# A two-layer diffusion trunk on one core: the second attention's context norm goes behind the first k product, the latent sums two tiles later, and the halves of the final norm get tiles of their own

## The chip, the cores and the metric

The kernel runs on one core of a Trainium2 chip. The metric is device time in microseconds (us) of one execution. TensorE (PE) does the matrix products, VectorE (DVE) and ScalarE (ACT) the elementwise work, GpSimd (POOL) a few additions and multiplications and some transfers, and SyncE (SP) issues most transfers. Each engine works through its own list of instructions in order; between engines an instruction waits for semaphores.

## The reference

512 latent tokens and 256 context tokens of 1024 features pass two layers. A layer is a modulated RMS norm, an attention with a gated residual, a second modulated norm, and a SwiGLU feed-forward part (2816 hidden) with a gated residual. The second layer gives no context out, so there the context is only normed and projected to keys and values. The output is the latent stream after a final RMS norm.

```python
def rmsnorm(x, g):
    y = xf * lax.rsqrt(jnp.mean(xf * xf, axis=-1, keepdims=True) + NORM_EPS)
    return y * g
...
h_x = modulate(rmsnorm(x, norm_g[layer, 0]), mod_x[0], mod_x[1])
h_c = modulate(rmsnorm(ctx, norm_g[layer, 0]), mod_c[0], mod_c[1])
...
    q_x, k_x, v_x = jnp.split(h_x @ w_in, [C_Q_COLS, C_Q_COLS + C_KV_COLS], axis=-1)
        kv_c = h_c @ w_in[:, C_Q_COLS:]
...
    x = x + mod_x[5] * swiglu(h_x, ffn_w1[layer], ffn_w3[layer], ffn_w2[layer])
return rmsnorm(x, final_g)
```

## The kernel before

Features lie on the 128 partitions, tokens along the row: a stream of 1024 features is eight tiles (KT = 8), 128 x 512 for the latents (`xr`, later `x1`) and 128 x 256 for the context (`cr`). For precision every operand of a large product is split into a high and a low part (`hb` holds both of a normed tile, `wh` and `wl` those of a weight tile), and a product is three matmuls per tile of the contraction (`mm3`, L205, lines L207 to L209). ACT makes the high part of a weight by a cast, DVE the low part by a subtraction.

Around the change three pieces of work follow each other.

*The end of the first feed-forward part* (`down_last`, L1301). PE makes eight latent tiles, then eight context tiles, each 128 x 256 from 12 matmuls (L1281 to L1283). DVE adds each to its residual (`to_residual`, L1275). After the third context tile (`m == 2`) `next_norm` (L1162) is written, the latents' norm: squares on ACT (L329, L332), additions on DVE (L338) and POOL (L336) into two running tiles `ns_a`, a sum over the partitions on PE by a matmul with ones (L309), then Ln, Exp and Square on ACT (L313, L315, L316) between three small operations on DVE (L314, L317, L318). `h_make` (L345) then gives each of the eight tiles its scale (L350, DVE), shift and high part (L351, ACT) and low part (L352, DVE). Behind the last context tile the same norm is written for the context, in six slices of one tile `q`, sums and `h_make` included.

*The beginning of the second attention* (from L1404). `k_x(0)` makes the first two key heads of the latents (24 matmuls of 512 columns from `hb`, L207 to L209); `v_part` makes the values, first of the latents (`g` = 1, 2), then of the context (`g` = 0), as 128 x 256 matmuls (L396 to L398); `k_c(0)` makes the first context keys, and `k_x(1)`, `k_c(1)` the rest. The weight tiles come in the order that `weights0` (L540) writes: `w_c[8]` for the first keys and `w_c[10]`, `w_c[11]` for the values, then `w_c[9]` for the other keys. Those of 8 and 10 are split right behind the last hidden tile (`behind_g`, L529); `w_c[11]` is split as usual. There are three buffers for split weight tiles, so `w_c[9]` is split when one of the first three is done with.

*The end of the kernel* (the second `down_last`, L1726). The output is made in two halves of 256 tokens: eight tiles of the first half, then eight of the second (12 matmuls each, lines L207 to L209), each added to its residual by DVE (L1693). `final_norm(0)` (L1712) is written behind the third tile of the second half, `final_norm(1)` behind the last. A final norm squares and sums like the others, multiplies each tile by its gain on ACT (L1720, into `fo`), and, when 1/rms is there, multiplies `fo` by it, five tiles on DVE and three on POOL (L1723), and stores them (L1724). Both final norms take their tiles from the same small set of tags of one pool (`npool`, L1568).

The order in which engines meet this work is not the order of the text: a scheduler places each instruction in the list of its engine at build time, by the text's order as priority and its own estimate of when the inputs are there. `tc.issue_after(z)` makes it place an instruction behind `z`; the chip itself does not wait there. Once placed, the lists are fixed.

## Time and profile before

| | |
|---|---|
| runs (3) | 1646.57, 1652.71, 1653.13 us; median 1652.71 us |
| profiled execution, its own time | 1649.52 us |
| its span, first to last instruction | 1647.7 us |
| PE busy | 1567.5 us (95%), 10222 matmul records |
| DVE busy | 1251.1 us (76%) |
| ACT busy | 749.2 us (45%) |
| POOL busy | 272.6 us (17%) |
| mean granted TensorE clock | 0.989 |
| HBM read, written | 160.45 MB, 4.86 MB |

Times in the profile count from the first instruction, so the span ends at 1647.7 us, and 1.8 us of the execution's own time lie around it. A row of the timeline gives start and duration, the engine, the line, what is written from what, and in brackets how long the engine had been idle before and what released it. A matmul's duration contains the time to drain; matmuls that follow each other start closer together than their durations say. The granted clock is 1.00 at full speed.

### The profile page before, as it was taken

Reading aid. Unit: us, or ns where it says so; the run is one execution under the profiler, and the core shown is the slowest. Engines: PE = TensorE matmul, PEld = TensorE weight load, DVE = VectorE, ACT = ScalarE, POOL = GpSimd, SP = SyncE. Lnnn points to the kernel's source line nnn. Section 1 sums busy time; section 2 is a strip of 40 time slices with the busy share of each in tenths; the row PEclk is TensorE's granted clock in tenths of the full one; section 3 lists DMA queues with packets and bytes.
Section 4 is the critical chain, followed back from the end, with each engine's and each line's share of the span. In section 5 each row is a group of like instructions: output and inputs, shape, how many; then the busy total and the mean of one; then the engine's idle time right before and its main releaser. Section 6 shows DMA issues by size and latency. Waiting matters only on the chain.

```text
span 1647.7 us, 26339 instructions
## 1 busy us (share of the span) xinstructions
PE 1567.5 (95%) x10222; PEld 1402.1 (85%) x10222; DVE 1251.1 (76%) x2155; ACT 749.2 (45%) x1326; POOL 272.6 (17%) x313
## 2 busy tenths in 40 slices
PE   5999998999999899999999998999999999999996
PEld 3798887877888789999999996977788799989896
DVE  4758698976576888879798879587665987869685
ACT  4446554556244423333434254356655552525243
POOL 2222222345010000010100001254322000000001
PEclk9999999999999999999999999999999999999998
DMA  9323254644225556675766762411010432323321
GB/s 340 100 58 89 80 157 131 189 133 119 69 64 131 155 163 160 159 199 159 193 182 170 201 173 94 101 54 40 14 39 25 156 128 78 127 74 95 120 73 52
DMA packets 69508, 199.52 MB, mean 121 GB/s; under 512 B 6932, under 2 KB 19380, under 8 KB 69384
## 3 DMA queue, kind: packets, MB, share of 16 engines
q1 hardware_dynamic: 59464, 164.40, 32.1%
q0 software_dynamic: 9344, 32.92, 9.4%
q8 instruction: 81, 1.33, 0.3%
q10 hardware_dynamic: 576, 0.52, 0.1%
q14 instruction: 43, 0.35, 0.1%
HBM read 160.45 MB, written 4.86 MB: 100 GB/s over the span
## 4 chain that ended last, share of the span: by engine, by line
PE 58%; issue 7%; DMA 6%; DVE 6%; ACT 2%; POOL 0%; DVEq 0%; SPq 0%; POOLq 0%; ACTq 0%
PE f L1250 4%; PE f L1251 4%; PE f L1249 4%; PE f L1653 4%; PE f L1652 4%; PE f L1651 4%; PE f L1281 3%; PE f L1282 3%; PE f L1283 3%; DMA wl<-raw 2%; PE lin L207 2%; PE t L1485 2%; PE lin L208 2%; PE lin L209 2%; PE f L1705 2%
## 5 line engine op out<-in xcount | busy, mean ns | idle before, releaser
L196 ACT ACTIVATE wh<-raw 128x1024 fp32r<-128x1024 f32 (+1 forms) x94 | 90.2, 976 | 233.9 <-DVE raw L500 124.4
L207 PE MATMUL lin<-hb,wh 128*128 128x512 f32 (+1 forms) x456 | 161.3, 354 | 8.5 <-DVE q L369 2.2
L208 PE MATMUL lin<-hb,wh 128*128 128x512 f32 (+1 forms) x456 | 159.4, 349 | 0.1
L209 PE MATMUL lin<-hb,wl 128*128 128x512 f32 (+1 forms) x456 | 158.3, 347 | 0.0
L197 DVE TENSOR_TENSOR wl<-raw,wh 128x1024 fp32r<-128x1024 f32 (+1 forms) x94 | 104.7, 1119 | 34.7 <-ACT wh L196 32.6
L269 DVE SCALAR_TENSOR_TENSOR junk<-raw,tables 128x1024 bf16<-128x1024 f32 x80 | 97.6, 1220 | 20.1 <-DMA raw<-in_ada_wT_dram 19.8
L202 POOL DMA_DIRECT2D wl<-raw x41 | 35.7, 871 | 458.6 <-ACT wl L201 421.6
L1281 PE MATMUL f<-g,wh 128*128 128x512 f32 (+1 forms) x304 | 103.4, 342 | 6.0 <-DVE q L1263 5.0
L207 PEld LDWEIGHTS lin<-hb,wh 128*128 128x128 f32 x456 | 86.1, 189 | 22.8 <-issue 3.0
L159 DVE TENSOR_TENSOR wl<-raw,wh 128x1024 fp32r<-128x1024 f32 x62 | 81.4, 1313 | 29.8 <-ACT wh L158 27.0
L1282 PE MATMUL f<-g,wh 128*128 128x512 f32 (+1 forms) x304 | 103.4, 341 | 0.0
L1283 PE MATMUL f<-g,wl 128*128 128x256 f32 (+1 forms) x304 | 101.9, 338 | 1.2 <-DMA wl<-raw 1.2
L1652 PE MATMUL f<-hb,wh 128*128 128x256 f32 x360 | 101.7, 283 | 0.0
L1651 PE MATMUL f<-hb,wh 128*128 128x256 f32 x360 | 101.4, 283 | 0.0
L1653 PE MATMUL f<-hb,wl 128*128 128x256 f32 x360 | 101.2, 283 | 0.0
L158 ACT CAST wh<-raw 128x1024 fp32r<-128x1024 f32 x62 | 64.9, 1047 | 77.5 <-PE lin L208 23.6
L1250 PE MATMUL f<-hb,wh 128*128 128x384 f32 x288 | 96.3, 335 | 1.1 <-DVE hb L197 1.1
L1249 PE MATMUL f<-hb,wh 128*128 128x384 f32 x288 | 96.4, 335 | 0.7 <-ACT hb L196 0.7
L1251 PE MATMUL f<-hb,wl 128*128 128x384 f32 x288 | 96.3, 334 | 0.3 <-DMA wl<-raw 0.3
L208 PEld LDWEIGHTS lin<-hb,wh 128*128 128x128 f32 x456 | 86.3, 189 | 11.0 <-issue 0.9
L209 PEld LDWEIGHTS lin<-hb,wl 128*128 128x128 f32 x456 | 86.2, 189 | 10.3 <-issue 0.3
L336 POOL TENSOR_TENSOR ns_a<-ns_a,ns_s 128x256 f32<-128x256 f32 (+1 forms) x16 | 17.3, 1084 | 442.7 <-ACT ns_s L332 434.4
(397 smaller groups left out, 4953.7 us busy)
## 6 DMA issues: line engine op xcount, KB each, us to landing
raw<-in_w_dram SPq DMA_DIRECT2D x132, 512.0 KB, 3.8
raw<-in_ada_wT_dram SPq DMA_DIRECT2D x80, 512.0 KB, 4.2
wl<-raw POOLq DMA_DIRECT2D x41, 512.0 KB, 6.4
raw<-in_w_ab_dram SPq DMA_DIRECT2D x24, 512.0 KB, 4.4
raw<-in_ada_w_dram SPq DMA_DIRECT2D x16, 512.0 KB, 9.5
k<-k SPq DMA_DIRECT2D x16, 384.0 KB, 6.0
raw<-in_w_c_dram SPq DMA_DIRECT2D x12, 512.0 KB, 4.3
nb<-in_na_bias_dram POOLq DMA_DIRECT2D x16, 256.0 KB, 3.8
```

The costliest lines, as they stand in the source:

```text
L207: nc.tensor.matmul(ps, wh(k), xh(k), start=k == 0, stop=False)
L208: nc.tensor.matmul(ps, wh(k), xl(k), start=False, stop=False)
L209: end = nc.tensor.matmul(ps, wl(k), xh(k), start=False, stop=k == n - 1)
L1249: nc.tensor.matmul(ps, wh(k), b[:, 0, :], start=k == 0, stop=False)
L1250: nc.tensor.matmul(ps, wh(k), b[:, 1, :], start=False, stop=False)
L1251: nc.tensor.matmul(ps, wl(k), b[:, 0, :], start=False, stop=k == 3)
L1281: nc.tensor.matmul(ps, hi, g[:, 0, cols[v]], start=first, stop=False)
L1282: nc.tensor.matmul(ps, hi, g[:, 1, cols[v]], start=False, stop=False)
L1283: nc.tensor.matmul(ps, lo, g[:, 0, cols[v]], start=False, stop=last)
L1651: nc.tensor.matmul(ps, wh(k), b[:, 0, :], start=k == 0, stop=False)
L1652: nc.tensor.matmul(ps, wh(k), b[:, 1, :], start=False, stop=False)
L1653: nc.tensor.matmul(ps, wl(k), b[:, 0, :], start=False, stop=k == 3)
```

## The change

Three things are moved; no operation is added or left out.

1. `next_norm` is written after the fifth context tile (`m == 4`), not the third. Its sums on PE come two tiles (24 matmuls) later.
2. Of the context's norm only squares and additions stay in `down_last`; their two running tiles lie in a residual buffer that is free by then (`spool0`). The sum on PE, 1/rms and `h_make` are written behind `k_x(0)`, with tiles of the attention's own pool. The split of `w_c[11]` gets its place behind the fourth latent `h_make`.
3. `final_norm` is cut in two. What multiplies by 1/rms and stores is now `put_out`, and `put_out(0)` is placed behind the last residual addition. The second half's norm gets its running tiles and its 1/rms from another pool (`spool`, tag `sum`), not from those of the first half.

```diff
-    def behind_g(raw):
+    def behind(act, dve, raw):
         hi, lo = S.part_tiles()
-        with tc.issue_after(g_made[0].ins):
-            nc.scalar.copy(hi, raw[0])
-        with tc.issue_after(g_made[1].ins):
-            nc.vector.tensor_sub(lo, raw[0], f32(hi))
+        with tc.issue_after(act.ins):
+            nc.scalar.copy(hi, raw)
+        with tc.issue_after(dve.ins):
+            nc.vector.tensor_sub(lo, raw, f32(hi))
         return hi, lo
...
         for j in (8, 10):
-            S.add_made([w_c[j]], behind_g)
-        for j in (11, 9, 0, 1, 2, 3, 4, 5, 6, 7):
+            S.add_made([w_c[j]], lambda raw: behind(*g_made, raw[0]))
+
+        S.add_made([w_c[11]], lambda raw: behind(*h_made[3 - KT], raw[0]))
+        for j in (9, 0, 1, 2, 3, 4, 5, 6, 7):
             S.add(w_c[j])
...
-                if m == 2:
+                if m == 4:
                     next_norm()
             q = q_tile()
-            pool = Carve([q[:, NC * i : NC * i + NC] for i in range(6)])
-            r = rstd_of(fps(), sq_sum(cr, pool), D, pool)
-            for k in range(KT):
-                h_make(k, hc[k], cr[k], r, 1, 0, 1, pool)
+            sums = [spool0[0][:, NC * i : NC * i + NC] for i in range(2)]
+            c_sums.extend(sq_sum(cr, Carve(sums + [q[:, NC * i : NC * i + NC] for i in range(2)])))
...
         k_x(0, w0)
+        r = rstd_of(linp(), c_sums, D, npool)
+        for k in range(KT):
+            h_make(k, hc[k], cr[k], r, 1, 0, 1, npool)
         wv = [tuple(wslice(t, 256) for t in S.next(1 - i)) for i in range(2)]
...
-        fo = []
+        fo, gains = [], []
+
+        def norm_tiles(i):
+            a = (spool[0], "sum", 2) if i else (fp, "s", 2)
+            return PoolMap(ns_a0=a, ns_a1=a, ns_s=(fp, "q", 2), ns_v=(fp, "s", 2), ns_y=a, ns_t=(fp, "s4", 1))
...
-            r = rstd_of(fps(), sq, D, npool)
+            gains.append((ts, rstd_of(fps(), sq, D, pool)))
+
+        def put_out(i):
+            ts, r = gains[i]
             for k in range(KT):
                 (nc.gpsimd if k in (1, 4, 7) else nc.vector).tensor_mul(ts[k], ts[k], r)
-                (nc.scalar if i and k % 2 else nc.sync).dma_start(out[:, k, c], ts[k])
+                (nc.scalar if i and k % 2 else nc.sync).dma_start(out[:, k, halves[i]], ts[k])
...
                     if ci and m == 2:
                         final_norm(0)
+            with tc.issue_after(end.ins):
+                put_out(0)
             final_norm(1)
+            put_out(1)
```

What the scheduler makes of it differs from before at two places only.

The first is PE's list at the step from the feed-forward part to the second attention. `f<-q,ones` is the context's sum and `hb_124`, `hb_125` are the first two of the eight normed tiles; L1282, L1283 are the last down product. Before:

```order
L1282 MATMUL f<-g,T 128x256
L1283 MATMUL f<-g,T 128x256
L309 MATMUL f<-q,ones 128x256 x2
L207 MATMUL t<-hb_124,wh 128x512
L208 MATMUL t<-hb_124,wh 128x512
L209 MATMUL t<-hb_124,wl 128x512
L207 MATMUL t<-hb_125,wh 128x512
L208 MATMUL t<-hb_125,wh 128x512
```

The changed kernel has from the same place on (line numbers are its own: L399 to L401 are the value matmuls, L312 the sum):

```order
L1290 MATMUL f<-g,T 128x256
L207 MATMUL t<-hb_124,wh 128x512
L399 MATMUL t<-wh,hb_124 128x256 x2
L208 MATMUL t<-hb_124,wh 128x512
...
L208 MATMUL t<-hb_125,wh 128x512
L209 MATMUL t<-hb_125,wl 128x512
...
L401 MATMUL t<-wl,hb_125 128x256
L312 MATMUL lin<-res,ones 128x256 x2
L207 MATMUL t<-hb_126,wh 128x512
```

The context's sum has moved from ahead of the first key matmul to behind the second normed tile, and the value matmuls of that tile, which stood behind the keys, are now mixed in: each normed tile is used by nine matmuls (three for keys, six for values) before the next is asked for. Further on, the values of the context stand among the first context keys, so the last 14 matmuls ahead of `k_x(1)` begin where `w_c[10]` is last read; before, 36 stood there.

The second place is DVE's list at the end of the kernel. `res` is the residual addition of one output tile, `ns_a` an addition of squares, `fo` the multiplication by 1/rms. Before:

```order
L318 SCALAR_TENSOR_TENSOR ns_y<-ns_t,ns_y 128x256
L1693 SCALAR_TENSOR_TENSOR res<-f,mod_117,res 128x256
L338 TENSOR_TENSOR ns_a<-ns_a,ns_s 128x256
L1723 TENSOR_TENSOR fo<-fo,ns_y 128x256 x5
L1693 SCALAR_TENSOR_TENSOR res<-f,mod_117,res 128x256
L338 TENSOR_TENSOR ns_a<-ns_a,ns_s 128x256
L1693 SCALAR_TENSOR_TENSOR res<-f,mod_117,res 128x256
L338 TENSOR_TENSOR ns_a<-ns_a,ns_s 128x256
L314 TENSOR_SCALAR ns_v<-f 128x256
```

In the changed kernel:

```order
L321 SCALAR_TENSOR_TENSOR ns_y<-ns_t,ns_y 128x256
L1701 SCALAR_TENSOR_TENSOR res<-f,mod_117,res 128x256
L341 TENSOR_TENSOR ns_a<-ns_a,ns_s 128x256
L1701 SCALAR_TENSOR_TENSOR res<-f,mod_117,res 128x256
L1740 TENSOR_TENSOR fo<-fo,ns_y 128x256 x5
L317 TENSOR_SCALAR ns_v<-f 128x256
```

The five multiplications of the first half stood ahead of the last two residual additions; they now stand behind the last one, ahead of the second half's `ns_v`. POOL's list has changed in the same way: its two additions for the second half now come ahead of its three multiplications for the first.

More of the change, by code (lines that the diff above doesn't have):

```diff
@@ L303, in load_rows @@
             nc.gpsimd.dma_start(cs[v], crow_dram[v : v + 1, :].to_broadcast([P, D]))
+    h_made = []
     def rstd_of(ps, accs, dim, pool):
@@ L351, in h_make @@
         act = nc.scalar.activation(h[:, 0, :], t, AF.Identity, bias=b, scale=1.0)
-        nc.vector.scalar_tensor_tensor(h[:, 1, :], t, b, f32(h[:, 0, :]), op0=ALU.add, op1=ALU.subtract)
+        h_made.append((act, nc.vector.scalar_tensor_tensor(h[:, 1, :], t, b, f32(h[:, 0, :]), op0=ALU.add, op1=ALU.subtract)))
         return act
@@ L564, in weights0 @@
         for j in (8, 10):
-            S.add_made([w_c[j]], behind_g)
-        for j in (11, 9, 0, 1, 2, 3, 4, 5, 6, 7):
+            S.add_made([w_c[j]], lambda raw: behind(*g_made, raw[0]))
+        S.add_made([w_c[11]], lambda raw: behind(*h_made[3 - KT], raw[0]))
+        for j in (9, 0, 1, 2, 3, 4, 5, 6, 7):
             S.add(w_c[j])
     spool0, tpool, small_parts = [], [], []
+    c_sums = []
     ada1 = [(l, s_, k) for l, s_ in [(0, 5)] + [(1, z) for z in range(6)] for k in range(KT)]
@@ L1692, in to_residual @@
         def to_residual(m, ps, c):
-            nc.vector.scalar_tensor_tensor(x1[m][:, c], ps, mod[1][:, 5, 0, m : m + 1], x1[m][:, c], op0=ALU.mult, op1=ALU.add)
+            return nc.vector.scalar_tensor_tensor(x1[m][:, c], ps, mod[1][:, 5, 0, m : m + 1], x1[m][:, c], op0=ALU.mult, op1=ALU.add)
         def down(js):
@@ L1708, in down @@
                     to_residual(4 * i + m, ps[m], slice(0, NX))
-        fo = []
+        fo, gains = [], []
+        def norm_tiles(i):
+            a = (spool[0], "sum", 2) if i else (fp, "s", 2)
+            return PoolMap(ns_a0=a, ns_a1=a, ns_s=(fp, "q", 2), ns_v=(fp, "s", 2), ns_y=a, ns_t=(fp, "s4", 1))
         def final_norm(i):
             c = halves[i]
-            sq = sq_sum([x1[k][:, c] for k in range(KT)], npool, apart=i == 1)
+            pool = norm_tiles(i)
+            sq = sq_sum([x1[k][:, c] for k in range(KT)], pool, apart=i == 1)
             ts = []
@@ L1735, in down_last @@
                     )
-                    to_residual(m, ps, c)
+                    end = to_residual(m, ps, c)
                     if ci and m == 2:
                         final_norm(0)
+            with tc.issue_after(end.ins):
+                put_out(0)
             final_norm(1)
+            put_out(1)
         for n, sg in enumerate(supers):
```

## Prediction

> **What bounds the kernel now.** I read the page first, then the timeline of PE around the two places that change, then a table of windows over PE's gaps there, and last DVE, ACT and POOL beside them.
>
> ```profile
> PE 1567.5 (95%) x10222; PEld 1402.1 (85%) x10222; DVE 1251.1 (76%) x2155; ACT 749.2 (45%) x1326; POOL 272.6 (17%) x313
> ```
>
> PE is the bound nearly everywhere, so only time in which PE stands still or is slowed can be gained. The windows (stretch, length, busy time of each engine, then the granted clock) show three such gaps:
>
> ```profile
> 1004.60:1007.25 2.65, 0.02 (x1) 0.00 (x0) 2.55 (x5) 1.86 (x3) 1.27 (x1) 1.00 0.00 0
> 1017.25:1022.75 5.50, 0.03 (x1) 0.00 (x0) 5.43 (x9) 3.01 (x6) 2.37 (x3) 0.68 0.51 153
> 1022.75:1026.00 3.25, 3.23 (x8) 2.58 (x9) 3.21 (x6) 1.83 (x4) 0.00 (x0) 0.50 0.21 83
> 1026.00:1050.96 24.96, 24.96 (x191) 24.06 (x189) 15.57 (x30) 10.69 (x19) 2.57 (x2) 1.00 0.04 9
> 1630.70:1634.25 3.55, 0.03 (x1) 0.00 (x0) 2.65 (x8) 2.17 (x6) 1.46 (x2) 0.91 0.68 232
> 1634.25:1637.25 3.00, 2.93 (x6) 1.85 (x6) 0.00 (x0) 0.12 (x2) 0.00 (x0) 0.50 0.09 31
> ```
>
> While PE waits (rows 1, 2 and 5) DVE is busy; behind the second and the third gap PE runs at half clock for some 3 us more (rows 3 and 6). PE's timeline names what it waits for:
>
> ```profile
> 1007.25 2.84 PE L309 MATMUL f<-norm,ones 128*128 128x512 f32 x6 [2.63 <-DVE norm L338]
> 1009.53 0.68 PE L1281 MATMUL f<-g,wh 128*128 128x256 f32 x1
> ...
> 1016.88 0.28 PE L1282 MATMUL f<-g,T 128*128 128x256 f32 x1
> 1017.00 0.28 PE L1283 MATMUL f<-g,T 128*128 128x256 f32 x1
> 1022.77 2.08 PE L309 MATMUL f<-q,ones 128*128 128x256 f32 x4 [5.50 <-DVE q L338]
> 1024.29 0.99 PE L207 MATMUL t<-hb,wh 128*128 128x512 f32 x1
> ...
> 1050.96 0.40 PE L207 MATMUL t<-hb,wh 128*128 128x512 f32 x1
> 1051.19 0.40 PE L208 MATMUL t<-hb,wh 128*128 128x512 f32 x1
> ...
> 1630.45 0.28 PE L209 MATMUL f<-g,wl 128*128 128x256 f32 x1
> 1634.28 2.08 PE L309 MATMUL f<-ns_a,ones 128*128 128x256 f32 x4 [3.55 <-DVE ns_a L338]
> ```
>
> All three waits are for additions of squares: the latents' (2.63 us), the context's (5.50 us), the second output half's (3.55 us). Matmuls of 256 columns follow each other at 0.12 us, those of 512 at 0.23 us, so a context tile or an output tile of 12 matmuls takes 1.44 us. The first `k_x(0)` matmul starts at 1024.29, `k_x(1)` at 1050.96; from 1026.00 to there PE never stands still.
>
> **The change part by part.** *The latent sums two tiles later.* The next two context tiles fill 2 x 1.44 = 2.88 us where PE waits 2.63, so PE would reach the sums at 1007.48, 0.23 us later than now, and find them done. What is late next is the latents' norm itself, which needs as long from the sums as before:
>
> ```profile
> 1014.34 1.41 DVE L350 SCALAR_TENSOR_TENSOR norm<-res,amod,csr 128x512 f32<-128x512 f32 x2
> 1015.66 0.87 DVE L1275 SCALAR_TENSOR_TENSOR res<-f,mod,res 128x256 f32<-128x256 f32 x2
> 1017.72 1.22 DVE L159 TENSOR_TENSOR wl<-raw,wh 128x1024 fp32r<-128x1024 f32 x1
> 1022.31 0.41 DVE L338 TENSOR_TENSOR q<-q 128x256 f32<-128x256 f32 x1
> 1029.06 0.75 DVE L352 SCALAR_TENSOR_TENSOR hb<-norm,mod,hb 128x512 fp32r<-128x512 f32 x1
> ```
>
> ```profile
> 1015.12 0.72 ACT L351 ACTIVATE hb<-norm,mod 128x512 fp32r<-128x512 f32 x1 [1.18 <-DVE norm L350]
> ```
>
> The first high part is there at 1015.84 now, so at about 1016.1 then. PE ends its last three tiles at 1007.48 + 2.28 (the sums, 1007.25 to 1009.53) + 4.32, plus some 0.4 for the slow first matmul behind the sums: 1014.3 to 1014.5. It waits some 1.7 us, in place of 5.50.
>
> *The context's norm behind the first k product.* `k_x(0)` and the values no longer stand behind the context's sum, so from 1016.1 PE works at the pace at which DVE hands over the eight normed tiles. DVE now needs 15.47 us for them (1014.34 to 1029.81). In between stand three context residuals, two additions of squares, the split of `w_c[11]` and the three operations of the context's 1/rms; two residuals (0.8 us) and one addition (0.4) come ahead now, the rest stays. So the last tile is there at 1014.57 + 14.3 = 1028.9. PE's own need is close to that: nine matmuls a tile, 3 x 0.23 + 6 x 0.12 = 1.41, times eight, and some 0.7 for the context's sum (half of the 1.52 that it takes at half clock from 1022.77 to 1024.29), give 12.0 us from 1016.1, or 1028.1. The context's sum itself is asked for at about 1019; its last residual comes right behind the first two L350, its last addition some 2 us later, at 1018.5, so it adds no wait; were it late, the six tiles behind it in PE's list would be.
>
> From the last normed tile to `k_x(1)` PE has 126 matmuls left, two of 512 columns and 124 of 256: 0.5 + 14.9 = 15.3 us. The context's sixteen DVE and eight ACT operations, now made in this time, must not hold it. They take
>
> ```profile
> L352 DVE SCALAR_TENSOR_TENSOR hb<-q,mod,hb 128x256 fp32r<-128x256 f32 x8 | 3.5, 483 | 0.7 <-ACT hb L351 0.7
> L350 DVE SCALAR_TENSOR_TENSOR q<-res,amod,q 128x256 f32<-128x256 f32 x8 | 3.5, 478 | 0.0
> ```
>
> ```profile
> 1041.34 1.40 DVE L369 SCALAR_TENSOR_TENSOR gk<-rt,gk 64x512 fp32r<-64x512 f32 x2 [2.86 <-ACT gk L366]
> ```
>
> 7.0 us of busy time on DVE, with some 3 for the key's rope and low parts among them (of which this row is half); that is done by about 1038.7, and the 54 matmuls ahead of the first context use last until 1035.5, the last context use comes near 1043. So it is hidden, with the first tiles ready at about 1030; without that cover it would cost up to 3 us. The added wait is the split of `w_c[9]`: its buffer comes free when `w_c[10]` is last read, 14 matmuls ahead of `k_x(1)`.
>
> ```profile
> 1046.72 1.05 ACT L158 CAST wh<-raw 128x1024 fp32r<-128x1024 f32 x1 [3.61 <-PE t L397]
> ```
>
> ```profile
> 1047.80 1.23 DVE L159 TENSOR_TENSOR wl<-raw,wh 128x1024 fp32r<-128x1024 f32 x1 [5.05 <-ACT wh L158]
> ```
>
> From the cast's start to the low part's end pass 2.31 us; 14 x 0.12 and the two matmuls that need only the high part cover 2.1. PE would wait 0.2 to 0.3 us; all of the attention stands behind that wait. `k_x(1)` then starts at 1028.9 + 15.3 + 0.3 = 1044.5, against 1050.96: 6.5 us. Bounds: 7.4, if DVE loses nothing to waits and the last tile is there at 1028.0; 5.3, if the paces of PE and DVE do not mesh and a tile of 1.2 us is lost. SP's list is not reordered here, and its loads behind the splits move along.
>
> *The final norm.* The tail of the second half:
>
> ```profile
> 1628.96 2.84 DVE L1723 TENSOR_TENSOR fo<-fo,ns_y 128x256 f32<-128x256 f32 x5
> 1631.72 0.47 DVE L1693 SCALAR_TENSOR_TENSOR res<-f,mod,res 128x256 f32<-128x256 f32 x1
> 1632.44 0.47 DVE L1693 SCALAR_TENSOR_TENSOR res<-f,mod,res 128x256 f32<-128x256 f32 x1
> 1637.75 0.42 DVE L314 TENSOR_SCALAR ns_v<-f 128x256 f32<-128x256 f32 x1 [3.53 <-ACT ns_t L313]
> 1639.65 3.34 DVE L1723 TENSOR_TENSOR fo<-fo,ns_y 128x256 f32<-128x256 f32 x5
> ```
>
> ```profile
> 1633.95 0.42 ACT L332 ACTIVATE ns_s<-res 128x256 f32<-128x256 f32 x1 [0.18 <-POOL ns_a L336]
> 1637.25 0.47 ACT L313 ACTIVATE ns_t<-f,epst 128x256 f32<-128x256 f32 x1 [2.88 <-PE f L309]
> ```
>
> ```profile
> 1628.02 2.49 POOL L1723 TENSOR_TENSOR fo<-fo,ns_y 128x256 f32<-128x256 f32 x3 [7.73 <-DVE ns_y L318]
> ```
>
> PE ends at 1630.73. The last residual waits on DVE behind the five `fo` until 1632.44, its square behind POOL until 1633.95, and the sums then run at half clock until Ln starts at 1637.25. With `fo` of the first half behind, and running tiles of their own, the last residual ends at 1631.2, its square at 1631.6, and the third sum, at full clock and with the other two done meanwhile, at 1632.2: Ln 5.05 us earlier. Then comes what was moved: five `fo` on DVE from 1631.2, ahead of `ns_v`, which could start at 1632.7.
>
> ```profile
> L1723 DVE TENSOR_TENSOR fo<-fo,ns_y x10: 411/682/956, 1629.0 to 1642.6; 128x256 f32<-128x256 f32 x10
> ```
>
> At 0.41 to 0.68 us each they end at 1633.3 to 1634.6. POOL's three (2.49 us) should start near 1629.6, so most of DVE's run alone; I take 1633.6, and with the three operations of 1/rms behind it (0.43 each) `fo` of the second half at 1634.9 to 1635.0 instead of 1639.65. That is 4.7 us, bounds 4.0 and 5.05. The stores of the first half move from 1628.8 to some 1631.5 and later. SP and the transfers are theirs alone until 1635, when the second half's first store is issued. The sum is 6.5 + 4.7 = 11.2 us.
>
> **The rivals.** *The clock falls in the new gap (B).* The slice of 1 us in which it fell:
>
> ```profile
> 1019.00:1020.00 1.00, 0.00 (x0) 0.00 (x0) 1.00 (x2) 0.42 (x1) 1.00 (x2) 0.59 0.52 33
> ```
>
> It fell at 1019.2, 1.9 us after PE stopped, yet not at all in the gap of 2.63 us. A gap of 1.7 us is just below both. If it falls, PE has half clock until about 3.2 us after it resumes (1022.77 to 1026.00), which costs up to 1.6 us, twice if it happens twice: gain 8.0 to 9.6, 1641.5 to 1643.1.
>
> *The same without end: slower (E).* PE, paced by DVE, pauses within every tile, and the clock stays at half through the whole stretch from 1016. Its work there, 24 matmuls of 0.23, 168 of 0.12 and 0.7 for the sum, is 26.4 us and takes 52.8 then; `k_x(1)` starts at 1068.9, 17.9 us late, and with the tail's gain the kernel is 13 us slower, 1664. It decides once half clock lasts over 2 x 11.2 = 22 us. Against it: in the attention PE pauses too, and the clock stays full.
>
> ```profile
> 1140.00:1160.00 20.00, 18.60 (x164) 14.73 (x159) 15.17 (x45) 15.44 (x45) 7.99 (x11) 1.00 0.03 13
> ```
>
> The Trainium skill, page "TensorE: Matmul & The Clock Gate", section "A second HAM failure mode: psum-queue depth-cycling", speaks for this one: a PE that micro-idles between groups of matmuls swings between half and full clock. By that rule the gain would shrink or turn; the row above does not bear it out, and I give it little.
>
> *DVE's `fo` run slowly beside POOL (C).* At 0.956 us each they end at 1636.0, `fo` of the second half starts at 1637.2, the tail gains 2.5, the whole 9.0: 1642.1. The Trainium skill's "GPSIMD Engine Reference", section "1. Specifications", says that GpSimd shares its SBUF interfaces with VectorE, with contention where a VectorE instruction has two SBUF inputs; `fo` has two, and the spread from 411 to 956 ns agrees. The order now puts the two engines' `fo` mostly one behind the other.
>
> *The head's gain is given back (D).* The attention would start early and then wait for a weight, so only the tail's 4.7 us are left: 1646.4, within 0.5%. Against it:
>
> ```profile
> sum 200.00, PE 195.20 PEld 155.95 DVE 139.38 ACT 117.92 POOL 76.38; mean PE 19.52 PEld 15.59 DVE 13.94 ACT 11.79 POOL 7.64
> ```
>
> In the 200 us from 1060 on PE works 195, so what it gains ahead of them is not waiting for anything else.
>
> **How the numbers follow.** The profiled execution took 1649.52 us (span 1647.7, 1.8 around it), 3.2 below the median of the runs, 1652.71; runs spread from 1646.57 to 1653.13. Against its own time the sum gives 1638.3. I start from the middle of profiled time and median, 1651.1: 1639.9. About 0.5%, 8.3 us, is what a measurement of this kernel tells from no change.
>
> Chances: forecast 0.66, B 0.14, C 0.07, D 0.09, E 0.04. The forecast's own range is 1634 (lowest run less 12.5) to 1644 (highest less 9.3). B and C lie in it; reaching towards D, 1634 to 1646 leaves out E, part of D and the tails. Faster by over 0.5%: nearly all of the forecast, most of B and C, 0.75. Within: D and the rest, 0.21. Slower: E, 0.04.
>
> **What would show it.** Right: the first sums' wait on PE gone; one wait of 1 to 2.5 us ahead of `k_x(0)`; PE 85 to 95% busy in the 13 us behind it; `k_x(1)` some 6.5 us earlier; at the end no gap over 1 us between the last product and the sums, those at full clock, and Ln within 2 us of PE's last product. Wrong: half clock behind 1016 (B, E), a PE wait at the context's sum, a wait of over 1 us at `k_x(1)`, or one of several us in the attention (D), `fo` of the first half lasting over 4 us (C).

## The result, and the profile after

| | before | after |
|---|---|---|
| runs | 8 | 8 |
| median | 1652.41 us | 1640.37 us |
| lowest, highest | 1646.57, 1654.53 us | 1638.59, 1646.68 us |
| profiled execution, own time | 1649.52 us | 1641.84 us |
| its span | 1647.7 us | 1640.1 us |
| ratio of after to before | | 0.9938, 95% interval 0.9923 to 0.9953 |

The ratio is 10.2 us of 1652.4 (7.8 to 12.7): faster by over 0.5% by its best value, with an interval that reaches down to 0.47%. The forecast was 1639.9, in a range of 1634 to 1646.

The page of after, answering to the row of before: PE has the same work, so it is busy for the same time in a shorter span.

```profile
PE 1569.4 (96%) x10222; PEld 1403.5 (86%) x10222; DVE 1252.1 (76%) x2155; ACT 748.6 (46%) x1326; POOL 270.4 (16%) x313
```

PE's timeline of after at the three waits (start, duration, engine, line, tiles, and in brackets how long PE had stood and for what). L312 is the sum with ones, L1290 the last down product, L354 and L355 the high and low part of a normed tile.

```profile
1009.25 2.84 PE L312 MATMUL f<-norm,ones 128*128 128x512 f32 x6 [0.45 <-DVE norm L341]
...
1016.12 0.28 PE L1290 MATMUL f<-g,T 128*128 128x256 f32 x1
1018.17 0.50 PE L207 MATMUL t<-hb,wh 128*128 128x512 f32 x1 [1.77 <-ACT hb L354]
1018.50 0.40 PE L399 MATMUL t<-wh,hb 128*128 128x256 f32 x2
1019.13 0.79 PE L208 MATMUL t<-hb,wh 128*128 128x512 f32 x1 [0.23 <-DVE hb L355]
...
1023.03 1.03 PE L312 MATMUL lin<-res,ones 128*128 128x256 f32 x4
...
1046.69 0.40 PE L207 MATMUL t<-hb,wh 128*128 128x512 f32 x1
1046.93 0.40 PE L208 MATMUL t<-hb,wh 128*128 128x512 f32 x1
1047.45 0.50 PE L209 MATMUL t<-hb,wl 128*128 128x512 f32 x1
...
1626.93 0.28 PE L209 MATMUL f<-g,wl 128*128 128x256 f32 x1
1627.92 1.13 PE L312 MATMUL f<-ns_a,ones 128*128 128x256 f32 x4 [0.70 <-DVE ns_a L341]
```

The waits of 2.63, 5.50 and 3.55 us are now 0.45, 1.77 and 0.70 us, and the context's sum (1023.03) waits for nothing.

Three lengths carry the rest of this text, since executions reach the changed place up to 7 us apart (in the fourteen traces the first context tile's product starts between 997.9 and 1005.2 us). The *stretch* runs from that product's start to the start of `k_x(1)`; the *middle* from there to the start of the last down product's last matmul; the *tail* from there to the end of the span. The span is given to 0.1 us, so a tail holds to 0.05.

| | before | after | difference |
|---|---|---|---|
| first context tile starts at | 1000.15 | 1001.45 | +1.30 |
| stretch | 50.81 | 45.24 | -5.57 |
| middle | 579.49 | 580.24 | +0.75 |
| tail | 17.25 | 13.17 | -4.08 |
| span | 1647.7 | 1640.1 | -7.60 |

### The profile page after: what moved, and what is told of

It reads as the page before. It is cut to its first block, busy times and chain, and to the rows that moved or that the text cites. A ratio compares the mean times of both kernels' runs of the same rounds, so it can differ in the third digit from the quotient of the medians.

```text
span 1640.1 us, 26336 instructions
## 1 busy us (share of the span) xinstructions
PE 1569.4 (96%) x10222; PEld 1403.5 (86%) x10222; DVE 1252.1 (76%) x2155; ACT 748.6 (46%) x1326; POOL 270.4 (16%) x313
## 4 chain that ended last, share of the span: by engine, by line
PE 59%; issue 6%; DVE 5%; DMA 5%; ACT 2%; POOL 0%; DVEq 0%; SPq 0%; POOLq 0%; ACTq 0%
PE f L1256 4%; PE f L1258 4%; PE f L1257 4%; PE f L1661 4%; PE f L1660 4%; PE f L1659 4%; PE f L1288 3%; PE f L1289 3%; PE f L1290 3%; PE lin L207 2%; PE t L1493 2%; PE lin L208 2%; PE lin L209 2%; PE f L1712 2%; PE f L1714 2%
## 5 line engine op out<-in xcount | busy, mean ns | idle before, releaser
L1290 PE MATMUL f<-g,wl 128*128 128x256 f32 (+1 forms) x304 | 102.1, 339 | 0.8 <-DMA wl<-raw 0.8
L159 DVE TENSOR_TENSOR wl<-raw,wh 128x1024 fp32r<-128x1024 f32 x61 | 80.2, 1315 | 26.2 <-ACT wh L158 23.4
L339 POOL TENSOR_TENSOR ns_a<-ns_a,ns_s 128x256 f32<-128x256 f32 (+1 forms) x16 | 16.2, 1012 | 446.7 <-ACT ns_s L335 440.4
```

The costliest lines, as they stand in the source:

```text
L1290: nc.tensor.matmul(ps, lo, g[:, 0, cols[v]], start=False, stop=last)
```

## The experiments

Stretch, middle and tail of every trace, with the ratio to the kernel before and its 95% interval:

| run | stretch | middle | tail | ratio |
|---|---|---|---|---|
| before | 50.81 | 579.49 | 17.25 | |
| before again | 52.48 | 579.51 | 17.33 | 1.0008 (0.9994 to 1.0023) |
| latent sums later only | 48.75 | 579.58 | 16.69 | 0.9962 (0.9947 to 0.9977) |
| context norm behind only | 45.82 | 579.88 | 16.12 | 0.9967 (0.9954 to 0.9980) |
| final norm only | 51.11 | 579.54 | 13.08 | 0.9965 (0.9951 to 0.9979) |
| head only | 44.42 | 580.28 | 16.22 | 0.9953 (0.9935 to 0.9971) |
| after | 45.24 | 580.24 | 13.17 | 0.9938 (0.9923 to 0.9953) |
| after, gap filled (14) | 44.51 | 579.98 | 13.10 | 0.9932 (0.9915 to 0.9950) |
| after, two squares apart | 44.62 | 581.18 | 12.65 | 0.9918 (0.9898 to 0.9938) |
| both of these | 44.75 | 579.99 | 12.58 | 0.9924 (0.9907 to 0.9942) |
| squares apart, `w_c[11]` free | 47.95 | 579.48 | 12.62 | 0.9945 (0.9932 to 0.9957) |
| squares apart, gap filled (7) | 44.12 | 581.52 | 12.60 | 0.9924 (0.9910 to 0.9937) |
| before, waits filled, order moved | 49.08 | 579.51 | 17.15 | 0.9986 (0.9972 to 1.0000) |
| before, waits filled, same order | 48.92 | 579.56 | 17.28 | 0.9982 (0.9969 to 0.9996) |

### The parts of the change alone

*The latent sums two tiles later, nothing else.*

```diff
-                if m == 2:
+                if m == 4:
                     next_norm()
```

> The kernel before with one edit: the latents' norm is written after the fifth context tile, not the third. Theory (the end of the head is set by DVE and by the context's sum on PE): the 2.63 us wait ahead of the latents' sums goes, but PE only comes earlier to the context's sum, which DVE finishes at the same time as before; the wait there grows from 5.5 to about 8 us. From the first context tile to the first matmul of the second k product 50.3 to 51.0 us (before 50.8), the whole kernel 0 to 0.5 us faster. Rival (each wait counts by itself): 2.6 us less in that stretch.

Measured: a stretch of 48.75 us, 2.06 less than before, and a ratio of 0.9962, 6.3 us where 0 to 0.5 was expected. The theory that this part alone would be eaten up by a longer wait at the context's sum is wrong. The wait became shorter, not longer. DVE's timeline of this run shows why (L1275 residuals, L159 the split of `w_c[11]`, L338 additions of squares, L350 the latents' scale; the last row is PE's):

```profile
1014.92 0.48 DVE L1275 SCALAR_TENSOR_TENSOR res<-f,mod,res 128x256 f32<-128x256 f32 x1
1015.31 1.22 DVE L159 TENSOR_TENSOR wl<-raw,wh 128x1024 fp32r<-128x1024 f32 x1
...
1018.11 0.42 DVE L338 TENSOR_TENSOR q<-q 128x256 f32<-128x256 f32 x1
1018.44 1.41 DVE L350 SCALAR_TENSOR_TENSOR norm<-res,amod,csr 128x512 f32<-128x512 f32 x2
1018.58 2.07 PE L309 MATMUL f<-q,ones 128*128 128x256 f32 x4 [4.99 <-DVE q L338]
```

The context's last addition now starts 18.8 us after the first context tile (1018.11 less 999.28); in before it was 22.2 (1022.31 less 1000.15). The scheduler had placed it ahead of most of the latents' tiles instead of between them. I had read PE's order and not DVE's.

*The context's norm behind the first k product, nothing else.* All of the change's second part, with `m == 2` as before:

```diff
-            r = rstd_of(fps(), sq_sum(cr, pool), D, pool)
-            for k in range(KT):
-                h_make(k, hc[k], cr[k], r, 1, 0, 1, pool)
...
         k_x(0, w0)
+        r = rstd_of(linp(), c_sums, D, npool)
+        for k in range(KT):
+            h_make(k, hc[k], cr[k], r, 1, 0, 1, npool)
```

> The kernel before with the context's norm behind the first k product and the split of the eleventh weight tile behind the fourth latent tile, but the latents' norm still written after the third context tile, and the final norm as before. Theory: PE waits 2.6 us at the latents' sums, then works its last three context tiles until the first normed tile is there, so the 1.8 us wait ahead of the first k product and the half clock behind it are gone; from the first context tile to the second k product 44 to 45 us, as in the changed kernel (44.7) or up to 0.7 us better. Rival (the two tiles' move gives 2.6 us of its own): 47.3 us.

Measured: 45.82 us, above the 44 to 45 of the theory and below the rival's 47.3; the wait at the latents' sums is 2.81 us, and none is left ahead of the first k product, which starts right behind the last down product.

```profile
1006.37 2.84 PE L312 MATMUL f<-norm,ones 128*128 128x512 f32 x6 [2.81 <-DVE norm L341]
...
1016.12 0.28 PE L1290 MATMUL f<-g,T 128*128 128x256 f32 x1
1016.24 0.39 PE L207 MATMUL t<-hb,wh 128*128 128x512 f32 x1
```

So nearly all of the stretch's gain needs this part, and the later latent sums add about one us to it.

*The final norm alone.* The kernel before with the change's third part (diff above, from `fo, gains` on).

> The kernel before with the final norm's edit alone. Theory (the two places are independent): from PE's last product to the end of the span 13 us as in the changed kernel, against 17.25 before; the whole kernel 3.5 to 4.7 us faster, ratio 0.997 to 0.998. Rival (the gain at the end exists only because the head starts it earlier, or stores collide): under 2 us.

*The head alone.* The change without its third part.

> The changed kernel with the final norm as before: both edits at the second attention's beginning. Theory: from the first context tile to the second k product 44.7 us as in the changed kernel, the end as before (17.25 us from the last product), the whole kernel 5.5 to 7 us faster than before, ratio 0.9958 to 0.9966; the gain holds through the attention. Rival (the gain is given back in the attention): under 3 us although the stretch itself is 6 us shorter.

Measured: the final norm alone leaves the stretch (51.11) and brings the tail to 13.08; the head alone brings the stretch to 44.42 and leaves the tail at 16.22, an us below the 17.25 of the first trace. In the traces the two parts do not touch each other. The times, 0.9965 and 0.9953, are both better than expected (0.997 to 0.998 and 0.9958 to 0.9966). They add up to 13.6 us, more than the 10.2 of the whole change, but within the intervals.

### How far the kernel before differs from itself

> The kernel before once more, nothing changed: how far one kernel differs from itself. The four kernels so far beat the kernel before in time by 6.0 to 8.6 us, while their own traces show less in the stretches that they change (2.1 to 6.4 us), and the profiled execution of before lies 3 us under the median of its own runs. If the profiled execution of before was merely a quick one, the ratio is 1.000 (0.9985 to 1.0015), the stretch from the first context tile of the last down product to the second half's first k product is again 50.8 us (50.3 to 51.3), the tail from the start of the last down product to the span's end 16.0 to 17.3 us, and the difference of this execution to the first lies elsewhere in the program. Rival: the stretch itself varies from one execution to the next by 2 us or more (49 or 53 us); then the 2.1 us that moving the latents' sums alone seemed to bring is no finding.

Measured: ratio 1.0008, and a stretch of 52.48 us, 1.67 more than in the first trace: more than the theory allowed, less than the rival. The cause stands in the first row: the same three sums behind nearly the same wait (2.81 us, 2.63 in the first trace) took 4.39 us in all here, 2.84 in the first trace. PE's row for the first two of these matmuls, then four slices of 1 us (length, busy time of PE, PEld, DVE, ACT, POOL, granted clock, DMA):

```profile
1008.97 2.08 PE L309 MATMUL f<-norm,ones 128*128 128x512 f32 x2 [2.81 <-DVE norm L338]
```

```profile
1008.00:1009.00 1.00, 0.03 (x1) 0.03 (x1) 0.90 (x3) 0.82 (x2) 0.27 (x1) 0.86 0.00 0
1012.00:1013.00 1.00, 1.00 (x4) 0.41 (x3) 0.00 (x0) 0.00 (x0) 0.00 (x0) 0.94 0.00 0
1025.00:1026.00 1.00, 0.00 (x0) 0.00 (x0) 1.00 (x3) 0.72 (x1) 0.00 (x0) 0.89 0.97 384
1029.00:1030.00 1.00, 1.00 (x5) 0.77 (x5) 1.00 (x3) 0.97 (x4) 0.00 (x0) 0.90 0.00 0
```

In these traces the clock has two values, 1.00 and 0.50, so a slice of 0.86 changed after 0.72 us, at 1008.72; the other three changes lie at 1012.12, 1025.78 and 1029.20. The steps between them are 3.40, 13.66 and 3.42 us: one, four and one times 3.41. All changes of the clock in an execution, from first to last, lie on one such grid: in this one the fall at 29.08 and that at 1636.76 are 1607.68 us apart, 471 times 3.4133. The grid starts elsewhere in each execution. The Trainium skill, page "TensorE: Matmul & The Clock Gate", section "What's actually happening" of its Part 1, has a free-running window of 3413 ns; by that rule the grid is just what one would see, and the traces agree.

This turns "does the clock fall after this wait?" into a question of where the grid lies. For each wait I laid the grid of its own execution over it and took how much of the grid window with most idle time PE stood:

| trace, wait | most idle in one window | clock fell |
|---|---|---|
| before again, latents' sums, 2.81 us | 2.56 of 3.41 us | yes |
| before, context's sums, 5.50 us (the window in which it began) | 1.91 | yes |
| squares apart, `w_c[11]` free, 1.56 and 1.70 us | 1.93 | yes |
| final norm only, latents' sums, 3.01 us | 1.86 | no |
| before again, context's sums (window in which it began) | 1.82 | no |
| after, ahead of `k_x(0)`, 1.77 us, and some short pauses | 1.82 | yes |
| before, latents' sums, 2.63 us | 1.72 | no |
| context norm behind only, latents' sums, 2.81 us | 1.68 | no |
| squares apart, ahead of `k_x(0)`, 1.77 us | 1.43 | no |
| head only, ahead of `k_x(0)`, 1.77 us, and some short pauses | 1.39 | no |

In these waits the line lies at just over half of a window, 1.8 to 1.9 us. Elsewhere in the same traces it is less sharp: the clock also fell behind windows with as little as 1.51 us idle, and stayed at 1.00 behind two with 1.92. So the idle share of a window decides it below 1.5 and above 1.9 us; between them it only says that a fall is possible. The Trainium skill, page "TensorE: Matmul & The Clock Gate", same section, has the clock low after an idle window; here half of one was enough.

### What the clock costs, and filling the waits

*After, with 14 matmuls of constants in the gap ahead of `k_x(0)`; then with 7.* `keep_busy(ps, n)` writes n matmuls of 128x128 constants, whose result is not used; each is two rows in the trace.

```diff
-        k_x(0, w0)
+        keep_busy(linp(), 14); k_x(0, w0)
```

> The changed kernel with 14 matmuls of constants (128x128 f32, their result is not used) between the last down product and the first k product, where PE stands for 1.77 us. In the changed kernel's trace the granted clock fell to 0.50 from 1019.0 to 1022.3 after that gap; with the old final norm the same head had the same gap and kept 1.00, and its stretch from the first context tile to the second half's first k product was 44.42 us against 45.24. Theory: the half clock costs 0.8 us of the stretch where it comes, since PE and not DVE then ends the first k product; with PE kept busy the clock stays at 1.00, the wait before the first k product shrinks to 0.1 to 0.3 us (its start does not move, 16.4 to 17.2 us after the first context tile), and the stretch is 44.2 to 44.7 us. Rival: the 0.8 us is something else (the spread of the stretch itself); then the clock stays at 1.00 and the stretch is 45.0 to 45.5 us all the same. Time: within 1 us of the changed kernel's 1640.4 by either, so the trace decides and not the time.

Measured: the clock stayed at 1.00, and the stretch is 44.51 us, against 45.24 in after, where it fell, and 44.42 and 44.62 in two executions with the same gap in which it did not. So the half clock of 3.4 us costs 0.6 to 0.8 us where it comes; in the three traces with the gap filled it did not come, in those without it came in one of three. A constants' matmul takes 0.22 us, so 14 of them outlast the gap, and `k_x(0)` starts 17.22 us after the first context tile, at the edge of what was expected and later than without them (16.4 to 16.7); the stretch is no longer for it. The time is not told apart from that of after (0.9932 and 0.9938), as it should be when the fall comes in only some executions.

> The changed kernel with the two squares apart and 7 constants' matmuls (about 0.22 us each, 1.5 us together) in the gap of 1.77 us ahead of the first k product, instead of 14, which took 3.0 us and put its start off by 0.6 to 0.8 us. Theory: the clock stays at 1.00 and the start stays at 16.4 to 16.7 us after the first context tile; the stretch is 44.2 to 44.5 us, no more than 0.3 us under that with 14 (44.5 and 44.75), since VectorE sets its end; tail 12.5 to 12.7 us. Rival: the start decides, and the stretch is 43.8 to 44.0 us. Time: 1637 to 1639.5 us by either.

Measured, together with the edit of the next section: `k_x(0)` starts at 15.73, earlier than the 16.4 to 16.7 expected, in part because the latents' sums did not wait in this trace; the stretch is 44.12, just under the theory's 44.2 to 44.5 and above the rival's 43.8 to 44.0. The time is no better than without the filling.

*Before, with both waits filled.*

```diff
-            r = rstd_of(fps(), sq_sum(xr, pool, apart=True), D, pool)
+            kp = fps(); keep_busy(kp, 11); r = rstd_of(kp, sq_sum(xr, pool, apart=True), D, pool)
...
-            r = rstd_of(fps(), sq_sum(cr, pool), D, pool)
+            kp = fps(); keep_busy(kp, 23); r = rstd_of(kp, sq_sum(cr, pool), D, pool)
```

> The kernel before with 11 matmuls of constants ahead of the latents' sums and 23 ahead of the context's sums (about 0.22 us each; their results are not used), where PE stands for 2.6 to 3.0 and 5.5 us. In all traces so far the clock's falls and returns lie on a grid of 3.413 us that runs through the whole execution, and it fell where PE was busy in less than about 45% of a grid window. In before's second execution such a fall in the first of these waits made the sums 4.39 us instead of 2.84 and the stretch 52.48 us instead of 50.81; after the second wait the clock was at 0.50 each time, and the context's sums took 2.08 us instead of 1.03. Theory: a part of what the change brings is that clock, not the waits themselves; with both waits filled the clock stays at 1.00, the context's sums take 1.0 to 1.1 us, the stretch is 48.3 to 49.8 us, and the time lies 2 to 4 us under the kernel before (a ratio of 0.9975 to 0.999): it also loses the executions with the slow first sums. Rival: VectorE alone sets the end of this stretch, and the clock there costs nothing; stretch 50.5 to 51.0 us, ratio 1.000.

This first run took banks of its own for the constants, and with that the scheduler put `k_x(0)` ahead of the context's sums (they start at 1031.22, 26.1 us after the first context tile instead of 22.6). Its 49.08 us are therefore not the clock's price alone, and the run was made again with the code shown here.

> The kernel before once more with 11 and 23 constants' matmuls (0.23 us each) ahead of the latents' and the context's sums, now written into the sums' own banks. In the run with banks of their own TensorE's order had changed as well: the first k product stood ahead of the context's sums, so that its 49.08 us of stretch did not tell the clock's cost. Here TensorE's order at both sums is that of the kernel before. Theory: with both waits filled the clock stays at 1.00; the context's sums take 1.0 to 1.1 us instead of 2.08, the nine matmuls behind them no longer run at half clock, the stretch from the first context tile to the second half's first k product is 48.0 to 49.8 us instead of 50.8 to 52.5, and the time lies 1.5 to 4 us under the kernel before (ratio 0.9975 to 0.999). Rival: the waits alone make the stretch, the clock is hidden behind VectorE: stretch 50.5 to 51.1 us, and the time differs from the kernel before by less than 1.2 us (the cost of the executions in which the clock falls at the latents' sums).

Measured: stretch 48.92 us, 1.9 and 3.6 less than the two traces of before, and a ratio of 0.9982, 3.0 us (0.7 to 5.1). Of the 1.9 us, 0.4 are there before the context's sums, which start 22.19 us after the first context tile instead of 22.62.

```profile
1002.25 2.62 PE L219 MATMUL f<-ones,ident 128*128 128x128 f32 x22
1004.70 2.74 PE L309 MATMUL f<-norm,ones 128*128 128x512 f32 x6
...
1014.47 5.29 PE L219 MATMUL f<-ones,ident 128*128 128x128 f32 x46
1020.13 1.13 PE L309 MATMUL f<-q,ones 128*128 128x256 f32 x4 [0.37 <-DVE q L338]
```

The context's sums take 1.13 us instead of 2.08. So of what the change brings, some 2 to 3 us were never the waits but the half clock behind them. It came behind the context's wait in all four traces that have this wait (before twice, latent sums later, final norm only), and behind the latents' in one of four. This may be part of why the later latent sums alone are worth more in time (6.3 us, interval 3.8 to 8.8) than one pair of traces shows (2.06): they remove the wait in which before again lost 1.7. The rest of that difference is not explained.

### What the tail fell short by

*After, with the last two squares of the second final norm summed by PE instead of the last one only* (`apart` is now a number):

```diff
-            if apart and k == KT - 1:
-                return accs + [sq]
+            if apart and k >= KT - apart:
+                accs.append(sq); continue
...
-            sq = sq_sum([x1[k][:, c] for k in range(KT)], pool, apart=i == 1)
+            sq = sq_sum([x1[k][:, c] for k in range(KT)], pool, apart=2 * i)
```

> The changed kernel, in whose second final norm the last two squares (not only the last) go to the sum over partitions by themselves: VectorE's last addition, which took 1.02 us instead of 0.42 beside GpSimd's three multiplies of the first half's outputs and held up the last residual, is gone, and TensorE adds one 128x256 tile more. Theory: that addition is what the tail fell short by. The last residual starts 0.3 us after the last down product's start instead of 0.86, the last square and the Ln 0.5 us earlier (Ln 2.0 to 2.2 us after the last product's start instead of 2.63), and the tail from the last product's start to the span's end is 12.5 to 12.8 us instead of 13.17. Rival: VectorE is slowed beside GpSimd whatever it does there; the residual of 0.47 us then takes about 1 us itself, and the tail stays at 13.0 to 13.3 us. The head is the changed kernel's: a stretch of 44.4 us where the clock stays, 45.2 where it falls.

After's tail on DVE, ACT and POOL (L1701 residuals, L341 the addition, L1740 `fo` times 1/rms, L316 Ln, L335 squares):

```profile
1626.84 1.02 DVE L341 TENSOR_TENSOR ns_a<-ns_a,ns_s 128x256 f32<-128x256 f32 x1 [0.54 <-ACT ns_s L335]
1627.79 0.47 DVE L1701 SCALAR_TENSOR_TENSOR res<-f,mod,res 128x256 f32<-128x256 f32 x1
1628.18 1.89 DVE L1740 TENSOR_TENSOR fo<-fo,ns_y 128x256 f32<-128x256 f32 x5
...
1631.96 3.35 DVE L1740 TENSOR_TENSOR fo<-fo,ns_y 128x256 f32<-128x256 f32 x5
...
1628.35 0.42 ACT L335 ACTIVATE ns_s<-res 128x256 f32<-128x256 f32 x1 [1.14 <-DVE res L1701]
1629.56 0.47 ACT L316 ACTIVATE ns_t<-f,epst 128x256 f32<-128x256 f32 x1 [0.39 <-PE f L312]
...
1626.15 2.29 POOL L1740 TENSOR_TENSOR fo<-fo,ns_y 128x256 f32<-128x256 f32 x3
```

POOL multiplies the first half's `fo` from 1626.15, 0.78 us ahead of the last product's last matmul, as forecast (1629.6, 0.85 ahead), since `put_out(0)` is behind the last residual only on DVE's list. What I had not seen is what runs on DVE then. Its addition of two tiles beside it takes 1.02 us; an addition two tiles earlier, without POOL, took 0.42. The last residual, its square and the sums wait behind it. With the addition gone, PE's and the other engines' rows read:

```profile
1628.15 0.28 PE L209 MATMUL f<-g,wl 128*128 128x256 f32 x1
...
1628.47 0.48 DVE L1701 SCALAR_TENSOR_TENSOR res<-f,mod,res 128x256 f32<-128x256 f32 x1 [0.95 <-PE f L209]
1628.87 2.23 DVE L1740 TENSOR_TENSOR fo<-fo,ns_y 128x256 f32<-128x256 f32 x5
...
1632.65 3.35 DVE L1740 TENSOR_TENSOR fo<-fo,ns_y 128x256 f32<-128x256 f32 x5
...
1630.25 0.47 ACT L316 ACTIVATE ns_t<-f,epst 128x256 f32<-128x256 f32 x1 [0.39 <-PE f L312]
...
1627.36 2.12 POOL L1740 TENSOR_TENSOR fo<-fo,ns_y 128x256 f32<-128x256 f32 x3
```

The residual comes 0.32 us after the last product's start (0.86 in after), Ln 2.10 (2.63), the second half's `fo` 4.50 (5.03), and the tail is 12.65 us: what the theory said. The rival falls: the residual runs beside POOL and takes its 0.48 us. It has one input in PSUM and one in SBUF; the slow addition had two in SBUF. The first half's five `fo`, which also have two there and now start while POOL is still multiplying, take 2.23 us instead of 1.89. The Trainium skill, page "GPSIMD Engine Reference", section "1. Specifications", names just this: VectorE and GpSimd share SBUF interfaces, with contention where VectorE has two SBUF inputs. The trace of after agrees, 1.02 against 0.42 us.

The middle of this run, 581.18 us, has 0.9 us too much: the clock fell once more, from 1278.0 to 1281.4, behind a wait of 1.40 us that every trace has. In the run with 7 constants it fell at 1133.2. Such draws are part of why one trace of a kernel lies some us from its median.

*Both edits together.*

> Both of the two edits before: constants' matmuls in the gap ahead of the first k product, and the last two squares apart in the second final norm. If each does what its theory says, the stretch at the attention's head is 44.2 to 44.7 us, the tail 12.5 to 12.8 us, and the time 0.5 to 1.3 us under the changed kernel's 1640.4, a ratio to the kernel before of about 0.993. If neither does, 45.2 and 13.1 us and no difference in time.

Measured: stretch 44.75, tail 12.58, a median of 1638.67 us. The tail is what was expected, the stretch 0.05 above the range, and the time is not told apart from that of the two squares apart alone (1637.69).

### The place of one split

*After with two squares apart, but the split of `w_c[11]` not placed behind the fourth normed tile.*

```diff
-        S.add_made([w_c[11]], lambda raw: behind(*h_made[3 - KT], raw[0]))
-        for j in (9, 0, 1, 2, 3, 4, 5, 6, 7):
+        for j in (11, 9, 0, 1, 2, 3, 4, 5, 6, 7):
             S.add(w_c[j])
```

> The changed kernel with the two squares apart, but the split of w_c[11] (a cast of 1.05 us on ScalarE and a subtraction of 1.2 us on VectorE) no longer placed behind the fourth normed tile: VectorE now does it ahead of the first two tiles' low parts. Theory: VectorE's work in the stretch is the same, only its order is other; the first k product starts 1.0 to 1.3 us later (17.6 to 18.0 us after the first context tile instead of 16.6), PE stands for about 3 us there and the clock falls in most executions, and the stretch is 44.5 to 45.8 us. The wait for w_c[9]'s split at the second k product (0.29 us) stays, and with it the 0.4 us that the changed kernel loses in the 20 us behind that product. Rival: the end of the stretch hangs on the first k product's start, and it grows by the whole 1.2 us to 45.8 to 46.5 us.

Measured: a stretch of 47.95 us, 3.3 more than with the split placed; both theories were too low. Stretches of this run, first around the two waits, then at half clock, then behind:

```profile
1015.00:1017.00 2.00, 0.74 (x3) 0.49 (x3) 2.00 (x4) 1.53 (x3) 1.06 (x2) 1.00 0.32 61
1017.34:1024.16 6.82, 5.49 (x18) 4.84 (x19) 5.68 (x10) 1.39 (x2) 0.00 (x0) 0.50 0.39 130
1024.16:1030.00 5.84, 5.84 (x39) 5.26 (x38) 4.70 (x10) 3.37 (x7) 0.00 (x0) 1.00 0.00 0
```

```profile
1016.24 0.50 PE L207 MATMUL t<-hb,wh 128*128 128x512 f32 x1 [1.56 <-ACT hb L354]
1018.67 0.80 PE L208 MATMUL t<-hb,wh 128*128 128x512 f32 x1 [1.70 <-DVE hb L355]
...
1023.11 1.55 PE L312 MATMUL lin<-res,ones 128*128 128x256 f32 x4
...
1025.21 0.42 DVE L317 TENSOR_SCALAR ns_v<-lin 128x256 f32<-128x256 f32 x1 [2.06 <-ACT ns_t L316]
```

`k_x(0)` does not start later (15.99 us after the first context tile); its second matmul waits another 1.70 us for the low part that DVE makes behind the split. The two waits together cross the line, the clock is at half for two grid windows, 6.82 us with 5.49 of work, which loses 2.7 us of PE, and DVE then stands 2.06 us for the context's sums. My theory had only the first wait and took DVE as the bound throughout. So in this trace the placing of this split is worth some 3 us, most of it by way of the clock. The other half of that theory fell too: the middle is 579.48, that of before. The scheduler's order ahead of `k_x(1)` is another here, 23 matmuls instead of 14 stand behind the last use of `w_c[10]`, and the wait for `w_c[9]` is gone.

## Why the prediction was right, and where not

*The stretch: right.* Forecast: `k_x(1)` at 1044.5 on before's clock, 44.35 us after the first context tile. Measured: 44.42 and 44.62 where the clock stayed, 45.24 in after, where it fell. The steps: wait for `k_x(0)` 1.77 us (forecast 1.7), no wait at the context's sum, 0.29 us at `k_x(1)` (`w_c[9]`, forecast 0.2 to 0.3), the last of the eight normed tiles 28.84 us after the first context tile (forecast 28.75). Two steps between were off and cancel: `k_x(0)` starts 16.72 us after the first context tile, 16.4 to 16.7 in the two other traces, where the forecast has 15.95 (in after the latents' sums still wait 0.45 us, in the others 0.15 to 0.34), and DVE then hands the eight tiles over in 13.67 us instead of 14.3. PE is busy for 97 to 98% of the 13 us behind `k_x(0)`, not for 85 to 95%. The forecast gain was 6.5 us; the difference of the means of three traces each (50.81, 52.48, 51.11 and 45.24, 44.42, 44.62) gives 6.7. It was right by its steps, but its base was one trace: the stretch of before is 50.8 or 52.5, as the grid falls.

*Rival B happened, and was priced twice too high.* The clock fell in the new gap in one of three traces, at 1018.94:

```profile
1016.40:1018.17 1.77, 0.00 (x1) 0.01 (x1) 1.77 (x4) 0.78 (x2) 1.09 (x2) 1.00 0.17 26
1018.17:1018.94 0.77, 0.73 (x3) 0.48 (x3) 0.77 (x2) 0.77 (x2) 0.00 (x0) 1.00 0.75 246
1018.94:1022.36 3.42, 3.23 (x11) 2.85 (x12) 3.38 (x7) 1.79 (x4) 0.00 (x0) 0.50 0.26 104
1022.36:1032.06 9.70, 9.70 (x62) 8.73 (x61) 9.23 (x18) 5.64 (x10) 0.00 (x0) 1.00 0.18 56
```

I had read the fall as a time since PE stopped (1.9 us in one gap, over 2.63 in another), which the two rows could not be made to fit. The share of a grid window fits both: 1.91 us idle in the window in which the long wait began, at most 1.72 in one window at the other. Price: up to 1.6 us forecast, 0.6 to 0.8 measured; it fits that DVE, busy for 3.38 of the 3.42 us at half clock, sets the pace there, but no run shows this apart. Rival E did not occur: the pauses behind `k_x(0)` are a few tenths each, and the clock was back after one window.

*The tail: the mechanism right, the term too large.* Forecast 4.7 us (bounds 4.0 and 5.05), measured 4.08 in this pair of traces and 3.7 over all of them, under the lower bound. Of the prediction's text the step that failed is "with `fo` of the first half behind, and running tiles of their own, the last residual ends at 1631.2 [...] Ln 5.05 us earlier". Ln came 4.17 us earlier against the last product: only DVE's `fo` were behind, and POOL's, though I had their start right, slowed DVE's addition ahead of the last residual. With that addition gone the second half's `fo` starts 4.50 us after the last product's last matmul; the forecast, 1634.9 to 1635.0 on before's clock, was 4.5. Rival C's mechanism was there, at another instruction than I had put it: the five `fo` took 0.38 us each. And 1.1 us of the old tail was the clock: where it had not fallen yet, the old tail is 16.1 to 16.2 us, and the gain is 3.0.

*What was not in the sum.* The middle: 0.75 us longer. Of this, 0.43 arise within the first 2.3 us behind `k_x(1)`: the wait for `w_c[9]`, 0.29, and the matmuls around it. In the small, this is rival D. The other 0.32 arise at one place, 184 us behind `k_x(1)`, where the weights of an attention score wait for ACT:

```profile
1230.37 0.30 PEld L1453 LDWEIGHTS s<-gk,gq 128*128 128x128 f32 x2 [0.35 <-ACT p L1462]
```

The traces of head only and of two squares apart have the same wait; before, and the traces with the gap filled, do not. Why it comes is open.

*The sum.* From all traces: stretch 6.7, tail 16.86 to 13.12 (seven traces with the old final norm, three with the new one), 3.7, less 0.7 in the middle: 9.7 us, against 10.2 (7.8 to 12.7) by the ratio. The forecast's 11.2 us, taken from 1651.1, gave 1639.9; the tail's excess and the base, 1.3 us under the median, nearly cancel. That the time met the median within 0.5 us is luck, better than its terms deserve.

## What to carry to other kernels

A PE wait costs more than its length: once PE stands for about half of a 3.41-us window, what follows is likely to run at half clock for one or two windows, so look at the granted clock behind each wait before pricing its removal, and take stretches from several traces, since the grid lies differently in each. When work is moved for one engine, read the order of all engines: in the first experiment DVE's reordering was the gain, and in the last a single split on DVE cost some 3 us, most of it by way of the clock. Work moved "behind" something on one engine is behind it on that engine's list only; here GpSimd started early and slowed the VectorE addition that the end waited for, and letting PE sum one more square took 0.5 us off the tail. That kernel has the lowest median of the study, 1637.69 us, though those with the gap filled as well (1638.44 and 1638.67) are not told apart from it.

## What was not expected of the hardware

- The clock's changes lie on a grid of 3.413 us through a whole execution (471 steps fit within 0.1 us). With the grid laid over all fourteen traces, from 60 us on and without the last 16 us: no window with PE idle for less than 1.5 us brought a fall, all 22 with more than 1.92 us did, and between 1.51 and 1.92 both were seen. After a fall the clock came back at the end of each window in which PE was busy for 2.87 us or more, and stayed low for another where it was busy for 2.80 or less.
- VectorE's addition of two 128x256 f32 tiles in SBUF took 1.02 us beside GpSimd's multiplications, 0.42 alone; its operation with one input in PSUM took 0.48 us either way.
- A 128x128 matmul of f32 constants took about 0.22 us, start to start, at full clock.
